# RMSNorm with swish: when SyncE issues the stores of each storing phase

## The chip, the cores and the metric

The kernel runs on one core of one Trainium2 chip. The core has several engines that work side by side: VectorE (DVE), ScalarE (ACT), GpSimd (POOL), TensorE (PE), and SyncE (SP), which here issues the transfers between the chip's main memory (HBM) and the on-chip memory (SBUF). The transfers themselves run on 16 DMA engines. The metric is the device time in microseconds (us), as the median of several runs; lower is better.

## The reference

The input x has 16 x 1024 rows of 512 float32 numbers. Each row is divided by its root mean square, multiplied by gamma, and passed through the swish function. The output has the same shape.

```
rms = np.sqrt(np.mean(x ** 2, axis=-1, keepdims=True) + eps)
x_norm = x / rms * gamma
return (x_norm * (1.0 / (1.0 + np.exp(-x_norm)))).astype(np.float32)
```

So 33.55 MB are read, 33.55 MB are written, and little is computed on each number.

## The kernel before, in words

The 16,384 rows are spread over the 128 partitions of the SBUF, 128 rows in each. In what follows "row" means one of these 128 places, which is one row of 512 numbers in every partition: 128 x 2 KB, 256 KB in all. Rows are grouped by 16 in HBM (`groups`, line 28), so that a partition's 16 rows of one group lie in one piece of 32 KB. A transfer of 16 rows is 4 MB, and each of the 16 DMA engines carries it as 8 packets of 32 KB, one for each of its 8 partitions, and a small packet that signals completion. A transfer of 8 rows has packets of 16 KB, one of 4 rows has packets of 8 KB.

The SBUF holds a ring of 96 rows (`xb`, line 76). All work is done in place there: a row is loaded, normalized, passed through swish and stored from the same place. The last 32 of the 128 rows take the places of the first 32, and so can be loaded only when those have been stored.

SyncE issues all large transfers from one queue, in the order of the list `order` (lines 34 to 37), in four stages:

- the loads of rows 0 to 95, in eight pieces (line 30); the first two of them are placed ahead of the rest of the program (`early`, lines 140 to 149)
- the stores of rows 0 to 31, in three pieces of 16, 8 and 8 rows
- the loads of rows 96 to 127, in pieces of 16, 8 and 8 rows (line 31)
- the stores of rows 32 to 127, in seven pieces

A store waits on SyncE until ScalarE has finished the rows that it takes (`store`, line 132; the semaphore `s_swish` counts units of four rows). A load of the third stage waits until the stores of the rows in its places have landed (`load`, line 121, lines 125 and 126). Since SyncE works in order, whatever stands behind a waiting instruction waits with it. The DMA engines serve the queue in the order in which the transfers were issued. Each transfer has a semaphore of its own (`ld`, `st`) that reaches 16 when all 16 engines have finished their shares.

Compute runs in 32 units of four rows. For each unit ScalarE squares the rows (`square`, two of them with the sum taken along), VectorE sums the other two (`sums`), GpSimd adds eps and raises to the power -0.5 (`power`), VectorE multiplies by that and by gamma (`norm`), and ScalarE applies swish (`swish`). ScalarE squares two units ahead of the one to which it applies swish. TensorE computes nothing: it waits for the loads in turn and counts the units that have landed into one semaphore for ScalarE (lines 156 to 159).

Of the kernel before, what the change touches and what calls it, by code (L numbers as in the profile page):

```python
# [9 lines left out]
def kernel(  # L10
# [7 lines left out]
    nc = tc.nc  # L18
# [8 lines left out]

    groups = [16] * 8
    ring = 96
    loads = [(0, 4), (4, 4), (8, 8), (16, 16), (32, 16), (48, 16), (64, 16), (80, 16)]  # L30
    loads += [(96, 16), (112, 8), (120, 8)]
    stores = [(0, 16), (16, 8), (24, 8), (32, 16), (48, 16), (64, 16), (80, 16)]
    stores += [(96, 16), (112, 8), (120, 8)]
    order = [("load", i) for i in range(loads.index((96, 16)))]
    order += [("store", t) for t in range(3)]
    order += [("load", i) for i in range(loads.index((96, 16)), len(loads))]
    order += [("store", t) for t in range(3, len(stores))]
    early = 2
    cn = 4
    n_sq = 2  # L40
# [46 lines left out]
    ld = [nc.alloc_semaphore(f"ld{t}") for t in range(len(loads))]  # L87
# [14 lines left out]
    def need(ins, sem, value):  # L102
        return ins.wait_op(sem, value, "sem-ge")

    def dram(ap, piece):
        a, n = piece
        g = max(g for g in range(len(groups)) if first[g] <= a)
        r = a - first[g]
        assert r + n <= groups[g], piece
        rows = ap[P * first[g] : P * (first[g] + groups[g])]  # L110
        return rows.rearrange("(p n) d -> p n d", n=groups[g])[:, r : r + n, :]

    def buf(piece):
        a, n = piece
        at = a % ring
        assert at + n <= ring, piece
        return xb[:, at : at + n, :]
# [3 lines left out]
    def load(i):  # L121
        a, n = loads[i]
        for u, (c, m) in enumerate(stores):
            over = c + ring < a + n and a < c + m + ring
            if over and u not in stored_by_sync:
                nc.sync.wait_ge(st[u], 16)
                stored_by_sync.add(u)
        return nc.sync.dma_start(
            out=buf(loads[i]), in_=dram(xf, loads[i])
        ).then_inc(ld[i], 16)  # L130

    def store(t):
        need(
            nc.sync.dma_start(out=dram(of, stores[t]), in_=buf(stores[t])),
            s_swish, ends[t],
        ).then_inc(st[t], 16)
# [11 lines left out]
        )  # L148
        entry.insert(at, ins)
    for what, t in order[early:]:  # L150
        load(t) if what == "load" else store(t)

    def take(queue, sem, n):
        need(queue.nop(nofuse=True), sem, n).then_inc(sem, -n)
# [151 lines left out]
```

## Time and profile before

| what | value |
|---|---|
| time, median of 3 runs | 160.66 us (160.58 to 160.77) |
| the profiled execution, its own time | 160.9 us |
| its span in the profile | 159.4 us |
| DMA packets and bytes | 3033 packets, 67.12 MB, mean 421 GB/s |
| first load issued, landed | 0.0 us, 4.8 us |
| first store issued | 30.09 us |
| loads of rows 96, 112 and 120 on issued | 71.31, 76.19 and 81.20 us |
| stores of the fourth stage issued | 81.58 to 140.49 us |
| last work of ScalarE ends | 140.46 us |

The span is the time that the profile covers, from the first instruction on. The profile gives each engine's busy time and share, the DMA share (how busy the 16 DMA engines were on average) and GB/s (what they moved). A stretch can show a DMA share a little over 1 and an uneven rate, because a packet is counted whole in the stretch in which it starts. "A <- B" in a list of waits means that A stood still until B released it; the three numbers are the total in us, how often, and the longest. SPq is SyncE's queue of instructions. Semaphore events give the moment at which each DMA engine's share of a transfer was signalled as landed.

### The profile page before, as it was taken

To read this page: it belongs to the slowest core of one execution; us is meant where nothing else is said; L and a number is where in the kernel's file an instruction comes from. 1 tells how busy PE (TensorE), PEld (TensorE's weight loads), DVE (VectorE), ACT (ScalarE), POOL (GpSimd) and SP (SyncE) were. 2 spreads that over 40 slices of the span, in tenths; PEclk is the share of its full clock that TensorE was granted. 3 is DMA by queue.
4 is the path that set the end of the run, shared out by engine and by line. 5 is a ranking of instruction groups with operands and counts; after the bars stand their busy time and mean duration, and the time that the engine had idled before them with its cause. 6 is when DMAs were issued, how large, how long until landed. Compare 5 with 4: busy or idle time off the path is not lost. (4 is left out here: it accounts for less than half of the span.)

```text
span 159.4 us, 900 instructions
## 1 busy us (share of the span) xinstructions
DVE 124.5 (78%) x162; ACT 129.6 (81%) x193; POOL 65.4 (41%) x70
## 2 busy tenths in 40 slices
DVE  0187969999999999999999999999999999700000
ACT  0939959999999999999999999999999995720000
POOL 1052545555555555555555555555555555000000
DMA  7999999999999999999999999999999999999896
GB/s 267 454 465 395 452 469 395 411 502 403 395 469 452 395 395 395 395 399 448 415 448 469 391 432 428 485 428 395 469 444 403 403 493 411 411 469 436 382 419 259
DMA packets 3033, 67.12 MB, mean 421 GB/s; under 512 B 341, under 2 KB 341, under 8 KB 345
## 3 DMA queue, kind: packets, MB, share of 16 engines
q1 hardware_dynamic: 3024, 67.11, 98.8%
q10 hardware_dynamic: 8, 0.01, 0.0%
q14 instruction: 1, 0.00, 0.0%
HBM read 33.56 MB, written 33.55 MB: 421 GB/s over the span
## 5 line engine op out<-in xcount | busy, mean ns | idle before, releaser
L223 DVE SCALAR_TENSOR_TENSOR xb<-xb,rstd,gamma_sb 128x512 f32 (+1 forms) x128 | 87.3, 744 | 0.0
L198 ACT ACTIVATE xb<-xb (+1 forms) x32 | 60.9, 1902 | 2.8 <-DVE xb L223 2.8
L213 DVE TENSOR_REDUCE ms<-sq 128x2 f32<-128x1024 f32 x32 | 39.2, 1224 | 14.0 <-ACT sq L192 10.7
L168 POOL TENSOR_SCALAR aeps<-ms 128x4 f32<-128x4 f32 x32 | 20.6, 644 | 65.6 <-DVE ms L213 65.6
L175 POOL TENSOR_TENSOR rstd<-aeps,neg_half 128x4 f32<-128x4 f32 x32 | 44.1, 1377 | 2.7
L186 ACT ACTIVATE junk<-xb 128x512 f32 (+1 forms) x64 | 38.6, 603 | 4.5 <-PEq L159 4.4
L192 ACT ACTIVATE sq<-xb 128x1024 f32 (+1 forms) x32 | 32.1, 1005 | 0.0
L186 ACT ACTIVATION_READ_ACCUMULATOR junk<-xb 128x1 f32 x64 | 11.9, 186 | 0.0
L206 ACT ACT_TABLE_LOAD x1 | 1.3, 1283 | 3.6 <-issue 3.6
L161 POOL MEMSET gamma<- 128x512 f32 x1 | 0.5, 524 | 1.5 <-POOLq L71 1.5
L233 DVE STREAM_SHUFFLE gamma_sb<-gamma 128x512 f32<-128x512 f32 x1 | 0.7, 721 | 0.0
L287 POOL MEMSET const-float32-0.0<- 128x1 f32 x1 | 0.1, 98 | 0.2 <-issue 0.2
L287 POOL MEMSET const-bfloat16-1.0<- 128x1 bf16 x1 | 0.1, 101 | 0.0
L287 POOL MEMSET const-uint8-127<- 128x1 uint8 x1 | 0.1, 101 | 0.0
L162 POOL MEMSET neg_half<- 128x4 f32 x1 | 0.1, 101 | 0.0
L287 POOL MEMSET const-float32-1.0<- 128x1 f32 x1 | 0.1, 99 | 0.0
L233 DVE LOAD_MASK_SELECT gamma_sb<-gamma x1 | 0.0, 14 | 0.0
## 6 DMA issues: line engine op xcount, KB each, us to landing
xb<-in_x_dram SPq DMA_DIRECT2D x6, 4096.0 KB, 33.4
out_dram<-xb SPq DMA_DIRECT2D x6, 4096.0 KB, 33.1
out_dram<-xb SPq DMA_DIRECT2D x4, 2048.0 KB, 27.9
xb<-in_x_dram SPq DMA_DIRECT2D x3, 2048.0 KB, 19.4
xb<-in_x_dram SPq DMA_DIRECT2D x2, 1024.0 KB, 5.8
gamma<-in_gamma_dram ACTq DMA_DIRECT2D x1, 8.0 KB
```

Source lines behind the costliest of these rows:

```text
L161: nc.gpsimd.memset(gamma4, 0.0).then_inc(s_zero, 1)
L162: nc.gpsimd.memset(neg_half, -0.5).then_inc(s_half, 1)
L168: nc.gpsimd.tensor_scalar(out=aeps[:, m, :], in0=ms[:, m, :], scalar1=eps_f, scalar2=None, op0=ALU.add,),
L175: nc.gpsimd.tensor_tensor(out=rstd[:, m, :], in0=aeps[:, m, :], in1=neg_half, op=ALU.pow),
L186: acc = nc.scalar.activation(out=junk[(k % turn) * (cn - n_sq) + j - n_sq], in_=rows(at + j, 1)[:, 0, :], func=AF.Square, scale=inv_d**0.5 ...
L192: nc.scalar.activation(out=sq[k % turn], in_=rows(at, n_sq), func=AF.Square, scale=inv_d**0.5,).then_inc(s_sq, 1)
L198: nc.scalar.activation(out=rows(at, cn), in_=rows(at, cn), func=AF.Silu),
L206: nc.scalar.preload_act_table_set("silu_and_others")
L213: nc.vector.tensor_reduce(out=ms[:, k % turn, 0:n_sq], in_=sq[k % turn], op=ALU.add, axis=mybir.AxisListType.X,),
L223: ins = nc.vector.scalar_tensor_tensor(out=row, in0=row, scalar=rstd[:, k % turn, j : j + 1], in1=gamma_sb, op0=ALU.mult, op1=ALU.mult,)
L233: nc.vector.stream_shuffle(gamma_sb, gamma4, [0] * 32), s_gld, 16
L287: nc = _bacc.Bacc("TRN2", target_bir_lowering=False, num_devices=1)
```

## The change

The last load of each loading stage is cut so that its final four rows are a transfer of their own: rows 80 to 95 go as 12 and 4 rows, and rows 112 to 127 go as 12 and 4 in place of 8 and 8. A new kind of step, "landed", is put into the order: SyncE waits until the transfer of 12 rows has landed, and only then goes on to the stores. One such step stands between the first loads and the first three stores, one between the second loads and the other seven stores. The stores, their sizes and their order stay as they are. Since rows 112 to 123 take the places of rows 16 to 27, their load now waits for both stores of 8 rows, where the load of rows 112 to 119 waited for one.

```diff
-    loads = [(0, 4), (4, 4), (8, 8), (16, 16), (32, 16), (48, 16), (64, 16), (80, 16)]
-    loads += [(96, 16), (112, 8), (120, 8)]
-    stores = [(0, 16), (16, 8), (24, 8), (32, 16), (48, 16), (64, 16), (80, 16)]
-    stores += [(96, 16), (112, 8), (120, 8)]
-    order = [("load", i) for i in range(loads.index((96, 16)))]
-    order += [("store", t) for t in range(3)]
-    order += [("load", i) for i in range(loads.index((96, 16)), len(loads))]
-    order += [("store", t) for t in range(3, len(stores))]
+    loads = [(0, 4), (4, 4), (8, 8), (16, 16), (32, 16), (48, 16), (64, 16), (80, 12), (92, 4)]
+    second = len(loads)
+    loads += [(96, 16), (112, 12), (124, 4)]
+    stores = [(0, 16), (16, 8), (24, 8)]
+    storing = len(stores)
+    stores += [(32, 16), (48, 16), (64, 16), (80, 16), (96, 16), (112, 8), (120, 8)]
+    order = [("load", i) for i in range(second)]
+    order += [("landed", loads.index((80, 12)))]
+    order += [("store", t) for t in range(storing)]
+    order += [("load", i) for i in range(second, len(loads))]
+    order += [("landed", loads.index((112, 12)))]
+    order += [("store", t) for t in range(storing, len(stores))]
...
     for what, t in order[early:]:
-        load(t) if what == "load" else store(t)
+        if what == "landed":
+            nc.sync.wait_ge(ld[t], 16)
+        else:
+            load(t) if what == "load" else store(t)
```

## The prediction

> **What bounds the kernel now.** I read the busy shares first, then the DMA queues, then SyncE's own waits, then the DMA rate in stretches, and last the trace's packets and semaphore events one by one. From the page:
>
> ```profile
> DVE 124.5 (78%) x162; ACT 129.6 (81%) x193; POOL 65.4 (41%) x70
> DMA  7999999999999999999999999999999999999896
> q1 hardware_dynamic: 3024, 67.11, 98.8%
> ```
>
> No engine fills the span, but SyncE's one queue (q1) keeps the 16 DMA engines busy for 98.8% of it. The reader should see that the transfers are the bound and that the queue is never empty: the DMA row has a 9 everywhere but in the first slice and near the end. SyncE's own waits say what holds the issues back:
>
> ```profile
> SPq L134 <- ACT xb L198: 97.5, 9, 25.2
> SPq L128 <- DMA out_dram<-xb: 34.1, 3, 24.9
> ```
>
> These 131.6 us of waiting cost nothing so long as issued transfers lie in the queue. The first store is issued at 30.09 and lands 41.2 us later; the last is issued at 140.49 and lands 18.8 us later. ScalarE ends at 140.46 and the span ends at 159.4, so compute has some 13 us to spare: 18.8 less the 4.9 that the last store of 8 rows itself takes and 0.65 for its completion. The chain of waits, which ends on ScalarE at 140.5, shows only who released the last issue; the queue set the end.
>
> So the time is bytes over rate, plus what the rate loses. I therefore asked for the DMA share and rate in stretches (columns: stretch, length, busy of DVE, ACT and POOL, clock, DMA share, GB/s):
>
> ```profile
> 0.00:1.00 1.00, 0.00 (x0) 0.00 (x0) 0.19 (x4) 1.00 0.00 0
> 31.10:40.80 9.70, 9.32 (x13) 9.70 (x16) 4.66 (x5) 1.00 1.00 432
> 40.80:50.50 9.70, 9.46 (x13) 9.70 (x15) 4.99 (x6) 1.00 1.00 432
> 57.00:60.60 3.60, 3.50 (x6) 3.60 (x7) 2.04 (x2) 1.00 0.97 291
> 96.00:99.60 3.60, 3.50 (x5) 3.60 (x7) 2.05 (x2) 1.00 1.03 441
> 99.60:103.20 3.60, 3.50 (x6) 3.60 (x7) 1.74 (x2) 1.00 1.01 437
> ```
>
> The steady rate is 432 GB/s. There is one hole: from 57.0 to 60.6 the engines are busy (0.97) but move 291 GB/s. The packets there say the same: a 32 KB packet takes 1.213 us everywhere, but the last two packets of each engine before its first store take 1.2 to 1.7 and 1.9 to 2.2. By the semaphore events, the 16-row loads land 9.71, 9.72 and then 10.62 us apart (31.57, 41.28, 51.00, 61.62). The hole costs 0.90 us, and it lies right at the first turn from loads to stores. At the second turn, near 99.6, there is none.
>
> **The change, part by part.** The sum is made against the profiled execution: span 159.4, 1.5 around it, 160.9 in all. That is 0.24 above the median of the runs, 160.66, so results against the median are 0.24 lower.
>
> *Split loads.* Rows 80 to 95 go as 12 and 4 instead of 16, rows 112 to 127 as 12 and 4 instead of 8 and 8. Per engine a load is 8 packets and a completion of 6 ns. Packets start 1.209 us apart at 32 KB, 0.607 at 16 KB, 0.306 at 8 KB; 24 KB is not in the trace, and halfway between 16 and 32 it is 0.908. First split: 8 x (0.908 + 0.306) + 0.012 = 9.72 against 9.68, +0.04. Second: 9.72 against 8 x 1.214 + 0.012 = 9.72, 0. One more issue on SyncE in the first stage (0.33 to 0.58 us each, all eight out by 4.84) is hidden by 46 us of queued loads. Sum +0.04.
>
> *First wait.* The three stores move from 30.09, 38.07 and 46.05 to when rows 80 to 91 have landed: 51.00 + 8 x 0.908 = 58.3. SyncE stands at this wait with the three stores and the three second-stage loads behind it. By then the stores' data are ready (the last was issued at 46.05 on its own wait). The loads behind wait for these stores to land anyway (71.29, 76.17, 81.19) and the queue is served in order, so nobody is later as long as the queue does not run dry. What hides the new latency is the 4-row load: 8 x 0.306 = 2.45 us per engine. What must fit in it is this. From the last byte to the landing event 0.35 to 0.37 (completion packet at 3.906, event at 4.251). Waking of SyncE, 0.02 (a store landed at 71.290, the load waiting for it was issued at 71.307), and 0.03 for a wait that is an instruction of its own, taken from the gap between the issues. From issue to first packet 1.02 to 1.39, which the first DMA shows (issued at 0, the row 0.00:1.00 above is empty, the engines start from 1.02 to 1.39). That is 1.44 to 1.81 after the last engine's share, so the last engine, which sets the end, has 0.64 to 1.0 us to spare. The earliest engine is 0.5 us ahead of it (spread of the 16 landings), so it has 0.1 to 0.5. Nobody runs dry: cost 0.
>
> Bounds for this price: from below 0 by the first DMA's row; from above by the rows that show slower starts. With the first DMA's slow first packets counted in, landing at 4.76 less 2.45 of data less 0.37 is 1.94, and the last engine still has 0.1 us. The gamma load on ScalarE's queue, issued at 2.47, shows its first packet only at 6.45, 4.0 us later, behind two stage-one loads: such a start would leave 4.0 + 0.42 - 2.45 = 2.0 us dry. I take the first, since it is SyncE's own queue and DMA shape and the gamma load stood between other queues' packets; 2.0 us per turn is kept for the range.
>
> The Trainium skill speaks against this change: its page "DMA: Bandwidth & Descriptors", section "Rules for kernel authors", says to issue a DMA early so that its fixed setup cost overlaps. The same page puts that cost at about 2 us, so two turns with nothing beside them would cost an estimated 4 us and give 164.7, and by its figure the 4-row load covers each.
>
> *Second wait.* The stores from row 32 on move from 81.58 and later to the landing of rows 112 to 123, about 98.3 (100.56 less 2.45, rounded up). The later ones wait for ScalarE anyway (109.92 to 140.49). Loads here spread 0.65 us, so the earliest engine has 0 to 0.35 us to spare and the last still 0.64 to 1.0. Cost 0, with the same upper bound. The load of rows 112 to 123 now needs two stores landed, so it is issued at 81.2 instead of 76.19; rows 96 to 111 keep the queue filled from 80.4 to 90. ScalarE needs those rows only near 117, so their landing 3 us later (98.3 instead of 95.66) costs 0.
>
> *The hole.* What the stores queued early can cost is at most what is lost ahead of them: 0.90. Nothing else on the page is odd at 57 us (the clock column is 1.00, ACT and DVE run as in the stretches before), and the hole sits on the two packets in front of the first store, in 4 of 159 us. With the stores out of the queue until 58.3, whose first packets could come at 59.3, I take it as gone: -0.90. The ends are 0 (it belongs to the moment, not to the queue) and -0.90; a gain on the second turn is excluded, since that shows 441 and 437 GB/s.
>
> Sum: 160.9 + 0.04 - 0.90 = 160.04, against the median 160.66 - 0.86 = 159.80.
>
> **The rivals.** *No change.* The hole stays, because it comes from something at that time or place which the change does not touch. For it: the second turn has stores queued since 81.58 and shows no hole, so early queuing alone does not make one. Against: it would be chance that it fell on that turn. Time 160.66 + 0.04 = 160.70.
>
> *Slower: the queue runs dry at the turns.* The price is 0.42 + start - 2.45 per turn for the last engine, so it decides from a start over 2.03 us. For it: a start beside running loads is seen only in the gamma load, at 4.0. Against: the first DMA's 1.02 to 1.39. With a start of 2.5 us it is 0.47 per turn: 160.70 + 0.94 = 161.64 if the hole stays too. At the gamma row's 4.0 it is 164.6.
>
> *The turn itself is what costs.* Loads and stores side by side lose 0.90 wherever stores arrive while loads are served; then both turns pay, the first as now and the second newly: 161.60. Against it is again the second turn's 441.
>
> **How the numbers follow.** Hole gone 0.41 (159.5 to 160.1: it may go in part); no change 0.32 (160.4 to 161.0); dry queue 0.19 (161 to 164.6, mostly below 162); costly turns 0.08. A measurement of this kernel can tell about 0.2%, 0.32 us. So faster 0.41, same 0.32, slower 0.27. The likeliest is 159.80. The range runs from 159.5, hole gone in full with a little more, to 161.6, the middle of the slower cases, which leaves some 0.15 out above and 0.05 below.
>
> **What the profile after would show.** Stores issued at about 58.3 and 98.3 and no longer at 30; 432 GB/s through 61 us in place of 291, and the first storing stage ending near 80.3 instead of 81.2; ScalarE's end unmoved at 140.5. A DMA share clearly under 0.9 in a stretch of 2 us around 60 or 100 would show a dry queue. A hole of the same size near 57 would show that the queued stores were not its cause. The prediction is wrong most simply if the hole was in one execution only and the timed runs never had it.

## The result and the profile after

The changed kernel takes 160.28 us (median, 160.13 to 160.51) where the kernel before takes 160.72 us (160.44 to 161.18) beside it. The ratio is 0.9973 with a 95% interval of 0.9966 to 0.9981: faster by 0.27%. The direction was forecast, and the size was about half of the forecast: 0.44 us gained in place of 0.86.

The profiled execution of the changed kernel has a span of 158.8 us and took 160.28 us. Its page, busy shares and the transfers:

```profile
DVE 124.5 (78%) x162; ACT 129.6 (82%) x193; POOL 65.4 (41%) x70
DMA  7999999999999999989999898999999999999896
q1 hardware_dynamic: 3168, 67.11, 99.0%
```

Compute is what it was, and the queue still fills the span. The two new waits stand at the top of SyncE's own waits (what was waited for, us in total, times, longest):

```profile
SPq L156 <- DMA xb<-in_x_dram: 69.7, 2, 52.9
SPq L138 <- ACT xb L205: 39.6, 4, 15.6
```

SyncE now stands 69.7 us at the waits for the loads, and the wait of the stores for ScalarE has shrunk from 97.5 to 39.6 us. The stores are issued at 58.46 and 98.21 us. The rates at the two ends of the loads, just behind the first of them (60.60 on) and at the turn from stores back to loads (77.40 on; stretch, length, busy of DVE, ACT and POOL, clock, DMA share, GB/s):

```profile
57.00:60.60 3.60, 3.50 (x6) 3.60 (x7) 2.04 (x2) 1.00 1.06 444
60.60:64.20 3.60, 3.52 (x5) 3.60 (x7) 2.05 (x2) 1.00 1.01 437
77.40:81.00 3.60, 3.46 (x6) 3.60 (x7) 2.04 (x2) 1.00 1.04 401
96.00:99.60 3.60, 3.46 (x6) 3.60 (x7) 2.01 (x2) 1.00 1.06 451
```

The hole at 57 us is gone: 444 GB/s in place of 291, and no dry queue behind it. New is 401 GB/s at a share of 1.04 near 79 us: packets that take longer than the usual 1.213 us (32 KB) and 0.611 us (16 KB), at the turn from the first stores to the second loads. In what follows they are called slow packets. The same stretch before has 469:

```profile
77.40:81.00 3.60, 3.46 (x5) 3.60 (x7) 2.04 (x2) 1.00 1.09 469
```

Where the time went is clearest in the landing events of the latest of the 16 DMA engines, since the latest engine sets the end. (It need not be the same engine all the time; that matters below.) The table has the four ends of the stages, from the semaphore events of the traces, in us. The second row of each kernel is a further profiled execution of the same code (the experiments below), and the last two kernels are experiments.

| kernel | rows 0 to 95 loaded | rows 0 to 31 stored | rows 96 to 127 loaded | last store |
|---|---|---|---|---|
| before | 61.62 | 81.19 | 100.56 | 159.33 |
| before, again | 61.48 | 81.09 | 100.37 | 159.08 |
| changed | 60.86 | 80.52 | 100.60 | 158.71 |
| changed, again | 60.78 | 80.58 | 100.38 | 158.69 |
| only the first wait | 60.81 | 80.70 | 102.22 | 160.40 |
| changed, rows 96 to 111 in 4 and 12 | 60.81 | 80.54 | 99.93 | 158.74 |

On the means of the two pairs, the changed kernel is 0.73 us ahead after the first loads, 0.59 after the first stores, level (0.02 behind) after the second loads, and 0.51 ahead at the end. So the gain is made at the first turn. Behind the turn at 80 us it is gone on the latest engine, and at the end most of it is there again; the last experiments show why.

### The profile page after: what moved, and what is told of

It is laid out like the page before. It is cut to its first block, busy times and chain, and to the rows that moved or that the text cites. A ratio compares the mean times of both kernels' runs of the same rounds, so it can differ in the third digit from the quotient of the medians.

```text
span 158.8 us, 905 instructions
## 1 busy us (share of the span) xinstructions
DVE 124.5 (78%) x162; ACT 129.6 (82%) x193; POOL 65.4 (41%) x70
## 5 line engine op out<-in xcount | busy, mean ns | idle before, releaser
L205 ACT ACTIVATE xb<-xb (+1 forms) x32 | 60.9, 1902 | 2.8 <-DVE xb L230 2.8
## 6 DMA issues: line engine op xcount, KB each, us to landing
out_dram<-xb SPq DMA_DIRECT2D x6, 4096.0 KB, 22.2
```

Of the source, the lines that this page charges most:

```text
L205: nc.scalar.activation(out=rows(at, cn), in_=rows(at, cn), func=AF.Silu),
```

## The experiments

Two theories were tested first. In the queue theory, stores that lie in the queue behind the loads slow the last packets of those loads. In the moment theory, the hole at 57 us is an event that the change does not touch. A third reading was tested with them, the lag theory: the gain comes from a shorter lag of the latest DMA engine behind the first at the end (1.38 us before, 0.81 after). All ratios are against the kernel before on the same chip. The diffs are against the changed kernel, where nothing else is said.

### The kernel before and the changed kernel, once more

No edit.

> The kernel before, unchanged. Queue theory (stores that wait in the queue behind the loads slow the last packets of those loads): the hole of about 0.9 us at 57 to 61 us is there again, on the last two packets of the load of rows 80 to 95, which lands 10.5 to 10.7 us after the load ahead of it; ratio 0.998 to 1.002. Moment theory (the hole is an event that falls where it falls): this profile shows no hole at 57 us, or one in another place, and the loads of rows 80 to 95 land 9.71 us after those ahead.

Measured: ratio 1.0001 (0.9992 to 1.0009). The load of rows 80 to 95 landed 10.50 us after the one ahead of it, and the hole is where it was, in a stretch of the same kind:

```profile
57.00:60.60 3.60, 3.50 (x6) 3.60 (x7) 2.04 (x2) 1.00 0.92 300
```

> The changed kernel, unchanged. First-turn theory (the first turn of the queue at which the next direction's transfers lie queued well ahead costs 0.8 to 0.9 us, once; a kernel that queues late at the first two loading ends pays it in small at the turn from stores to loads at 80 us): no hole at 57 to 61 nor at 97 to 100 us, slow packets at 78 to 81 us that put the latest DMA engine 0.7 to 1.0 us further back, ratio 0.9965 to 0.998. Chance theory: the slow packets at 78 to 81 us are missing or elsewhere.

(Its expectation names the theory that the parts of the change alone, told below, had suggested.) Measured: ratio 0.9972 (0.9960 to 0.9984). There is no hole at the two loading ends:

```profile
57.00:60.60 3.60, 3.50 (x6) 3.60 (x7) 2.04 (x2) 1.00 1.04 437
```

There are slow packets at 78 to 81 us. Behind them the load of rows 96 to 111 lands 10.05 us after the last store on the latest engine, 0.4 us more than a load of 16 rows should take. That is less than the 0.7 to 1.0 that I expected, and less than the 0.6 to 0.7 of the first profile (10.34 us). The hole and its absence come back with the kernel: the moment theory falls.

### The parts of the change alone

Only the cut of the loads:

```diff
-    order += [("landed", loads.index((80, 12)))]
-    order += [("landed", loads.index((112, 12)))]
```

> The loads are cut as 12 and 4 rows, both waits are left out, so the stores queue early again. Queue theory: the hole before the first store is back, time equal to before plus 0.04 us, ratio 0.999 to 1.002. If cutting the loads into smaller packets is what took the hole away: ratio about 0.9973, like the changed kernel. Moment theory: ratio anywhere in 0.997 to 1.002 and a hole that does not sit at the turn.

Only the first wait:

```diff
-    loads += [(96, 16), (112, 12), (124, 4)]
+    loads += [(96, 16), (112, 8), (120, 8)]
-    order += [("landed", loads.index((112, 12)))]
```

> Only the first wait, with rows 80 to 95 as 12 and 4; rows 112 to 127 as 8 and 8 and their stores queued early as before. Queue theory: the whole gain, ratio 0.9965 to 0.998, since the second turn showed no hole. If the second wait holds the gain (by a shorter lag of the latest DMA engine in the last storing stage, 1.38 us before and 0.81 after): ratio 0.999 to 1.002 and a lag of 1.3 us or more at the end.

Only the second wait:

```diff
-    ... (64, 16), (80, 12), (92, 4)]
+    ... (64, 16), (80, 16)]
-    order += [("landed", loads.index((80, 12)))]
```

> Only the second wait, with rows 112 to 127 as 12 and 4; rows 80 to 95 in one load and the first three stores queued early as before. Queue theory: the hole at 57 to 61 us is there, ratio 0.999 to 1.001. Lag theory: ratio about 0.9975 and a lag of the latest engine of about 0.8 us at the end instead of 1.38.

Measured: the cut alone 1.0000 (0.9991 to 1.0008), the first wait alone 1.0029 (1.0005 to 1.0052; single times from 160.23 to 162.38), the second alone 1.0004 (0.9995 to 1.0013). No part alone gains, and the first wait alone loses. The lag theory falls as well: with the second wait alone the lag at the end is 1.33 us, where it asked for 0.8. The rates at the first turn, with only the cut and with only the second wait:

```profile
57.00:60.60 3.60, 3.50 (x6) 3.60 (x7) 2.04 (x2) 1.00 0.88 278
57.00:60.60 3.60, 3.50 (x6) 3.60 (x7) 2.04 (x2) 1.00 0.96 300
```

and, with only the first wait, at the first turn and at the second:

```profile
57.00:60.60 3.60, 3.50 (x6) 3.60 (x7) 2.04 (x2) 1.00 1.04 437
96.00:99.60 3.60, 3.47 (x5) 3.60 (x7) 2.05 (x2) 1.00 1.05 355
```

This is the most telling pair of the study. The first wait takes the hole away at 57 us, as the queue theory has it, but the hole then stands at 97 us, before the second turn, where the kernel before has none although its stores lie in the queue there in just the same way. On the latest engine it costs 1.5 us there: the load of rows 120 to 127 lands 6.35 us after the one ahead, in place of 4.89. This is one execution, and one of the slow ones among the twelve timed (161.97 us, median 161.12); the fastest, at 160.23, took no longer than the changed kernel, so how large the hole at 97 us is in the others is not known. So I was wrong to expect the whole gain from the first wait. The theory that replaces the first one, tested below: the hole is paid once, at the first turn from loads to stores at which the stores have been queued well ahead. Both waits are needed, since each alone leaves one such turn.

### How early is too early

The first wait moved 10 us and 5 us ahead of the turn:

```diff
-    order += [("landed", loads.index((80, 12)))]
+    order += [("landed", loads.index((64, 16)))]
```

> Like the changed kernel, but the first wait is for rows 64 to 79, so the first three stores are queued at 51 us, 10 us before the turn in place of 2.4. If it matters only that stores lie in the queue when the last load packets are served: the hole of 0.8 to 0.9 us is back at 58 to 61 us, ratio 0.999 to 1.002. If it takes longer queueing, or stores issued one by one while loads run (30, 38 and 46 us before): no hole, ratio about 0.9973.

Cut and wait at eight rows in place of four, at both turns:

```diff
-    ... (64, 16), (80, 12), (92, 4)]
+    ... (64, 16), (80, 8), (88, 8)]
-    loads += [(96, 16), (112, 12), (124, 4)]
+    loads += [(96, 16), (112, 8), (120, 8)]
```

> Like the changed kernel with eight rows left to land in place of four (loads cut 8 and 8), so stores lie queued about 5 us ahead of the turn. If 5 us is already early: the hole is back at 57 to 61 us, ratio 0.999 to 1.001. If it takes between 5 and 10 us: no hole there, ratio 0.9965 to 0.998.

Measured: 1.0004 (0.9996 to 1.0013), and 0.9991 (0.9982 to 0.9999). In both profiles the hole is back. On the latest engine it is 0.69 us in the first (the last load lands 3.17 us after the one ahead, in place of 2.48) and 0.74 in the second (5.63 in place of 4.89). With the stores queued at 51 us, and at eight rows left:

```profile
57.00:60.60 3.60, 3.50 (x6) 3.60 (x7) 2.04 (x2) 1.00 0.88 298
57.00:60.60 3.60, 3.50 (x6) 3.60 (x7) 2.04 (x2) 1.00 1.07 373
```

Five us ahead (55.95 issued, 60.9 to 61.5 landed) is already early. Whether the stores came there one by one from 30 us on or together at 51, the hole is there.

No rows left to land at all, the queue dry at both turns:

```diff
-    order += [("landed", loads.index((80, 12)))]
+    order += [("landed", loads.index((92, 4)))]
-    order += [("landed", loads.index((112, 12)))]
+    order += [("landed", loads.index((124, 4)))]
```

> Like the changed kernel, but each wait is for all rows of the loads, the last four too, so the queue runs dry at both turns. By the start of the first DMA (0.35 to 0.37 to the landing event, 0.05 to the issue, 1.02 to 1.39 to the first packet) the latest engine stands still 1.4 to 1.8 us per turn: 2.9 to 3.6 us above the changed kernel, 163.2 to 163.9, ratio 1.015 to 1.020. If a start beside the queue takes 4.0 us as the gamma load did: 8 us above.

Measured: 163.94 us, ratio 1.0196 (1.0183 to 1.0209), 3.66 us over the changed kernel. At the turns and at the stores' end:

```profile
60.00:62.50 2.50, 2.40 (x4) 2.50 (x3) 0.81 (x2) 1.00 0.50 213
101.50:104.00 2.50, 2.50 (x4) 2.50 (x6) 2.04 (x2) 1.00 0.54 226
79.40:82.40 3.00, 2.86 (x5) 3.00 (x3) 1.03 (x3) 1.00 1.19 393
```

A share of 0.50 and 0.54 is a dry queue. The latest engine lands its first 16 stored rows 11.21 and 11.22 us after the loads, 1.54 and 1.55 us late, within the 1.44 to 1.81 that the prediction put together from the first DMA's start; the gamma load's 4.0 us was not the measure. These two starts make 3.1 of the 3.7 us. By the landings, about 0.3 us of the rest is lost at 80 us, before the turn from stores to loads, where a hole now stands (393 GB/s at 1.19), and the other 0.3 in the first loads and the last storing stage.

### Is it paid once

A store of 4 rows, queued at 16.4 us between the loads of the first stage, in the kernel before (its diff is shown) and in the changed kernel:

```diff
-    stores = [(0, 16), (16, 8), (24, 8), ...
+    stores = [(0, 4), (4, 12), (16, 8), (24, 8), ...
-    order = [("load", i) for i in range(loads.index((96, 16)))]
+    order = [("load", i) for i in range(5)]
+    order += [("store", 0)]
+    order += [("load", i) for i in range(5, loads.index((96, 16)))]
```

> The kernel before, with the store of rows 0 to 15 cut into 4 and 12, and the small one put into the queue after the load of rows 32 to 47, so that the first turn from loads to stores comes near 31 us and is only 4 rows long. If the hole is paid once, at the first turn with queued stores: slow packets of 0.7 to 0.9 us at 28 to 33 us and none at 57 to 61 us, ratio 0.999 to 1.003. If every long storing stage that follows a long loading stage pays it: the hole at 59 to 64 us stays, with or without a smaller one at 30 us, ratio 1.000 to 1.006.

> The changed kernel with the same small store early in the queue. If the hole is paid once: slow packets at 28 to 33 us, and after that no slow packets at 78 to 84 us either, ratio 0.999 to 1.002, the gain lost. If the early small store costs nothing and the waits do the rest: ratio about 0.9975, with slow packets again at 78 to 84 us.

Measured: 1.0020 (1.0011 to 1.0029) and 1.0026 (1.0015 to 1.0037). In the first of them, ahead of the small store and ahead of the large ones:

```profile
28.00:31.60 3.60, 3.50 (x6) 3.60 (x7) 1.96 (x2) 1.00 0.96 291
57.00:60.60 3.60, 3.50 (x6) 3.60 (x7) 2.04 (x2) 1.00 1.01 437
```

One store of 1 MB, queued early, draws the hole to 28 us, 30 us ahead of its old place, with 1.2 us on the latest engine (10.88 us between two loads in place of 9.71). The long storing stage that follows at 64 us then costs nothing, though its stores lie in the queue since 30 to 46 us. The second kernel shows 291 GB/s in the same stretch, and its waits then gain nothing:

```profile
28.00:31.60 3.60, 3.50 (x6) 3.60 (x7) 1.86 (x2) 1.00 1.06 291
```

Slow packets at 78 to 81 us stay there (3.5 us beyond the usual time, summed over the 16 engines, against 5.9 and 4.2 in the two profiles of the changed kernel), which I had not expected. That the large hole is paid once, at the first early-queued turn, is shown by this pair and by the first wait alone, with one profile of each. Why once, these runs do not say.

The slow packets at 80 us are another matter. Here is the same sum for every profile, two of the kernel before and of the changed one and one of each other (us beyond the usual time of a packet's size, for packets over it by more than 0.05). They go with the time at which the first large stores, those of 8 rows or more, are issued, and not with the hole:

| kernel | these stores issued from | before the first turn | at 80 us | before the second turn |
|---|---|---|---|---|
| before, and again | 30 | 17.0, 13.1 | 0, 0 | 0, 0.7 |
| cut alone | 30 | 12.6 | 0 | 0.2 |
| second wait alone | 30 | 15.2 | 0 | 0.1 |
| first wait 10 us ahead, 5 us ahead | 51, 56 | 10.1, 11.2 | 0, 0 | 0, 0.1 |
| small early store, kernel before | 30 | 16.4 (at 28 us) | 0.1 | 0.1 |
| small early store, changed kernel | 62 | 22.2 (at 28 us) | 3.5 | 0 |
| changed, and again | 58 | 0.1, 0.1 | 5.9, 4.2 | 0.2, 0.1 |
| first wait alone | 58 | 0 | 4.9 | 12.7 |
| dry at both turns | 61 | 0 | 13.2 | 0 |

Every kernel whose first large stores wait for 58 us or later has slow packets at 80 us, whether it has paid the hole or not, and no other has more than 0.1. So they come with the late issue, as a price of the first wait, and are not simply the hole that has moved. The kernels of the next two sections agree: 0.1 with stores issued from 22 us, 3.4 to 8.0 with stores issued at 58 us.

### The queue without compute

The transfers alone, in the order of the kernel before and of the changed kernel; all compute and the load of gamma are left out, and the stores wait for their rows' loads (the same edit in both):

```diff
-        need(
-            nc.sync.dma_start(out=dram(of, stores[t]), in_=buf(stores[t])),
-            s_swish, ends[t],
-        ).then_inc(st[t], 16)
+        a, n = stores[t]
+        for i, (c, m) in enumerate(loads):
+            if c < a + n and a < c + m and i not in landed:
+                nc.sync.wait_ge(ld[i], 16)
+                landed.add(i)
+        nc.sync.dma_start(out=dram(of, stores[t]), in_=buf(stores[t])).then_inc(st[t], 16)
```

> The transfers of the kernel before alone: all compute and the load of gamma are left out, each store waits for its rows to land and stores them as loaded. If the hole is the DMA queue's own matter: it is there before the first store at 57 to 61 us with 0.7 to 0.9 us, and the latest engine's lag in the last storing stage may be gone; ratio 0.995 to 1.000. If the compute engines' use of the SBUF makes it: no hole, ratio 0.990 to 0.995.

> The transfers of the changed kernel alone: all compute and the load of gamma are left out, each store also waits for its rows to land and stores them as loaded. Against the transfers of the kernel before alone (159.99). If the loss at the turn from stores to loads is the DMA queue's own: slow packets at 78 to 81 us and a latest engine 0.4 to 0.7 us further back after it, so 159.6 to 159.9. If that loss needs the compute engines beside it: no slow packets there, 159.2 to 159.4, the whole 0.7 gained.

Measured: 159.99 us, 0.9952 (0.9938 to 0.9966), and 159.20 us, 0.9908 (0.9892 to 0.9924). The first turn of the one and of the other (of the busy columns, only POOL's is left):

```profile
57.00:60.60 3.60, 0.00 (x0) 1.00 0.90 300
```

```profile
57.00:60.60 3.60, 0.00 (x0) 1.00 1.06 444
```

The hole is the queue's own: it stands there with no compute engine at work. And without compute the change gains 0.79 us, nearly what was forecast. Slow packets at 78 to 79 us stay in the second kernel (4.2 us summed over the 16 engines), but its latest engine does not fall back: it stands at 99.95 us at the end of the second loads, 0.3 us behind the middle one, and at 158.07 at the last store. My expectation had slow packets and a latest engine further back together, or neither. In the first, too, the latest engine holds its place in the last storing stage (0.69 us between first and last landing at the stage's start, 0.79 at its end, against 0.65 and 1.38 in the kernel before). In these two profiles, then, no engine falls back without compute beside it.

### Two versions that try to gain the rest

The same idea at the turn from stores to loads: the last store of the first stage cut in 4 and 4, and the second loads issued when the first of these has landed:

```diff
-    stores = [(0, 16), (16, 8), (24, 8)]
+    stores = [(0, 16), (16, 8), (24, 4), (28, 4)]
     order += [("store", t) for t in range(storing)]
+    order += [("stored", stores.index((24, 4)))]
...
+        elif what == "stored":
+            nc.sync.wait_ge(st[t], 16)
+            stored_by_sync.add(t)
```

> The changed kernel, with the same idea at the turn from stores to loads: the store of rows 24 to 31 is cut in two of four rows, and the loads of rows 96 on are issued when the store of rows 24 to 27 has landed (about 78 us), not at 70.6 us. First-turn theory: no slow packets at 78 to 81 us, loads of rows 96 to 127 landed 0.3 us (median engine) to 0.9 us (latest) earlier, ratio 0.993 to 0.997 unless the latest engine then falls back in the last storing stage as in the kernel before (0.7 us), which gives 0.996 to 0.998. If the stores' later landing leaves the queue dry there: 0.2 to 1 us slower than the changed kernel, 0.998 to 1.004.

Measured: 160.32 us, 0.9981 (0.9968 to 0.9993), with single times from 160.06 to 160.99: no gain on the changed kernel. The slow packets are still there (380 GB/s at a share of 1.04; 8.0 us in sum), though the loads were issued only at 77.8 us:

```profile
79.40:82.40 3.00, 2.87 (x4) 3.00 (x4) 1.04 (x3) 1.00 1.04 380
```

So my hope that a late issue clears this turn too was wrong.

Smaller packets behind that turn:

```diff
-    loads += [(96, 16), (112, 12), (124, 4)]
+    loads += [(96, 4), (100, 12), (112, 12), (124, 4)]
```

> The changed kernel with the load of rows 96 to 111 cut into 4 and 12, so the packets just behind the turn from stores to loads are of 8 KB. If the loss there falls on the first load packets (the latest engine's first 32 KB packet took 1.96 us in place of 1.21): a smaller loss, 159.9 to 160.2. If it falls on the last store packets, whatever comes behind: 160.2 to 160.4, as the changed kernel.

Measured: 160.29 us, 0.9976 (0.9966 to 0.9986), the changed kernel's time. Yet the table shows that here the latest engine passes the second loads at 99.93 us, 0.6 us ahead of the changed kernel. In the last storing stage the latest engine then falls back step by step: its 16-row stores land 9.91, 9.85, 9.84 and 9.79 us apart until compute ends near 140 us, and 9.69 after; in the first profile of the changed kernel they land 9.72, 9.66, 9.65, 9.66 and 9.70 apart. The end is the same. The changed kernel has this falling engine too; it is only not the latest. The stretches between the five landings of 16-row stores in the last stage, in us:

| kernel | which engine | the first three, beside compute | the last |
|---|---|---|---|
| before | latest | 9.84, 9.87, 9.77 | 9.72 |
| before | middle | 9.66, 9.66, 9.65 | 9.68 |
| changed | latest | 9.66, 9.65, 9.66 | 9.70 |
| changed | second latest | 9.86, 9.87, 9.77 | 9.70 |
| only the first wait | latest | 9.67, 9.69, 9.67 | 9.69 |
| only the first wait | second latest | 9.87, 9.85, 9.79 | 9.69 |
| changed, rows 96 to 111 in 4 and 12 | latest | 9.85, 9.84, 9.79 | 9.69 |

So two different engines compete for the last place. One falls back beside compute in each of these kernels. Another one loses 0.4 to 0.7 us to the slow packets at 80 us in the changed kernel and in the one with only the first wait (the load behind them lands 10.05 to 10.34 us after the last store in place of 9.7), and keeps its pace in the last storing stage. (The table goes by rank; the packets of one engine, each of which starts within some ns of the end of the one before, give the same two engines.) In the first profile of the changed kernel the second of them ends last, at 158.71, and the falling one at 158.61; in the further profile they change places on the way, and the falling one ends last, at 158.69. The cut of this experiment spares the one and leaves the end to the other. Neither version beats the changed kernel.

## Why the prediction was right or wrong

*What bounds the kernel* was right. Compute left out altogether saves 0.48%; the rest is the queue.

*Split loads, +0.04 us* agrees with what was measured, as far as it can be told: the cut alone is 1.0000, with an interval of 0.0009 (0.14 us) to either side, and 12 and 4 rows land in 9.78 us where 16 take 9.71.

*The waits cost nothing* was right in what it worked out, the start of the stores. They were issued at 58.46 and 98.21 (58.3 and 98.3 forecast). No engine ran dry at the first turn, and at the second only the earliest few, for 0.1 us at most, which the end does not feel. The start of 1.44 to 1.81 us was confirmed in sum by the kernel that lets the queue run dry (1.54 and 1.55; its first packets come 0.84 to 0.99 us after the issue, where the first DMA had 1.02 to 1.39), so the upper bound from the gamma load was far too high, and the rival of a dry queue falls. The Trainium skill's rule to issue early ("DMA: Bandwidth & Descriptors", "Rules for kernel authors") agrees with the dry kernel, where the uncovered start cost 1.5 us at each turn. The page's 2 us, from which the prediction estimated 164.7, are a fit for transfers issued from GpSimd; the dry kernel took 163.94. The measurement decides for the changed kernel, where a later issue with cover was faster (ratio 0.9973).

But 0 was wrong as the whole price of the first wait: it brings the slow packets at 80 us.

So two steps of the sum failed, *The hole is gone, -0.90* in its size, while its mechanism held, and the 0 for the first wait. Three things are in it:

- The 0.90 was read from one execution that was itself 0.24 us slower than the median; in the other one the hole is 0.79. Over the two pairs of profiles the first loads land 0.73 us earlier, the cut of the loads included.
- "A gain on the second turn is excluded", because that turn shows no hole, misread it. The second turn was free only because the first had paid. With the first wait alone the hole moves there, so the second wait, which I costed at 0, holds a part of the gain that the first cannot keep without it.
- No term was set for the turn from stores to loads at 80 us, where every kernel whose first large stores wait until 58 us has slow packets. Up to the landing of the first stores they cost the changed kernel 0.14 us, and one engine up to 0.7 us more in the load behind.

At the end 0.51 us of the 0.73 is left, where the sum had 0.86. The falling engine, last in the kernel before at 159.33 and 159.08, ends at 158.61 and 158.69, which is 0.55 earlier: it has lost 0.18 of the 0.73, nearly all of it by the landing of the first stores. The last few hundredths are the other engine's, which ends 0.10 later in one profile of two. The timed runs gain 0.44. Why the late issue makes packets slow at 80 us stays open.

*No change* (the rival) rested on the second turn as evidence that early queueing alone makes no hole. The evidence was true and the conclusion not: history matters. *The turn itself costs, both turns newly* falls, since no hole stands at either loading end of the changed kernel.

## What to carry to other kernels

On a kernel bound by one transfer queue, look at the packets just before the queue first turns from loads to stores: on this one, stores queued 5 us or more ahead cost 0.7 to 0.9 us there, once, and stores issued with 2.5 us of loads still to come made no hole there. The later issue had its own smaller price at the next turn, so the cure is worth less than the hole. A stage that shows no loss may owe that to an earlier stage that has paid, so a cure must be tried at every such turn together, not at the one that shows the loss. And the end is set by the latest DMA engine, so a saving is to be followed on the late engines from stage to stage, not on the mean rate; and since the latest one can change on the way, the second latest has to be watched too.

## What was unexpected of the hardware

In the profiles the large hole stands at most once, and it moves: to 28 us with a small early store, to 97 us with the first turn spared. With both turns spared it is gone, and the slow packets at 80 us that come with the first wait have less than half its sum (5.9 and 4.2 us against 17.0 and 13.1; 13.2 where the queue ran dry). What in the DMA engines or the memory does this is open. One of the 16 DMA engines falls back while compute runs: in the kernel before, its 16-row stores in the last stage land about 9.85 us apart while the middle engine's land 9.66 apart, and once compute has ended, or in the kernels without compute, the two go at the same pace. Why it is one engine was not settled. In the kernel with only the first wait the latest engine is 2.2 us behind the first one and stays there from 102 to 160 us: that is another engine, and the falling one does not catch up with it.
